# A hybrid mLSTM and attention block on one core: sweep order of the input projection, gate sums moved to TensorE, head norms moved to VectorE

## The chip, the cores and the metric

The kernel runs on one core of a Trainium2 chip. A core has TensorE (PE in the profile; its weight loads are PEld), VectorE (DVE), ScalarE (ACT), GpSimd (POOL) and a queue engine SyncE (SP), which here issues every DMA. All weights lie in HBM in float32 and are read once per launch, 313.81 MB in all. The metric is the device time of one launch in microseconds; smaller is better. Times are given as the median of several executions. One further execution was profiled.

## The reference

One transformer-like layer on 256 tokens of width 2048, in float32:

```
mod = silu(c) @ w_ada + b_ada -> shift1, scale1, gate1, shift2, scale2, gate2   (each 2048 wide)
h   = rms_norm(x, norm1_w) * (1 + scale1) + shift1
mq, mk, mv, mo, mi, mf, dq, dk, dv = split(h @ w_in)
h_ml = rms_norm(mlstm_chunkwise(silu(conv(mq)), silu(conv(mk)), mv, gates(mi, mf))) * sigmoid(mo)   (4 heads)
dq, dk = rope(rms_norm(dq)), rope(rms_norm(dk))
o_da = rms_norm(diff_attention(dq, dk, dv, lam))      (8 heads, two softmax maps each)
x = x + gate1 * (concat(h_ml, o_da) @ w_out)
h = rms_norm(x, norm2_w) * (1 + scale2) + shift2
g, u = split(h @ w_gate_up);  x = x + gate2 * ((silu(g) * u) @ w_down)
```

The kernel computes the mLSTM of a head as one masked 256 x 256 product with a running maximum. Nothing of what is computed differs between the two versions but the order of sums and the way a reciprocal root is refined.

## The kernel before

**Ticks.** The large products are cut into 392 ticks. A tick is 256 rows by 512 columns of weights, 0.524 MB. ACT makes the high part `wh` (line 542), DVE the rest `wl = raw - wh` (line 552), and TensorE runs 12 products of 512 columns, three for each of two weight rows blocks and two token halves: high by high, high by low, low by high (lines 581 to 583). The input projection takes 96 ticks, the output projection 32, the gate and up projection 176, the down projection 88. The order of the ticks is fixed when the program is made.

**Sweeps.** The input projection has 12 column groups: `DQ`, `DK`, `DV` with two groups each, `MQ`, `MK` with one each, `MV`, `MO` with two each. A group needs eight steps of 256 rows, and step p needs `h0_p`, the normed and modulated piece p of x, which in turn needs the column pair p of scale1 and shift1. So the groups are not done one by one but in sweeps (lines 48 to 55): all 12 groups for step 0, all for step 1, ten groups for steps 2 and 3 (`LATE[FIRST:]` leaves out `DV`), then the six `EARLY` groups for steps 4 to 7, `DV` for steps 2 to 7, and the other four for 4 to 7. At the end of every visit to a group, `project_done` (line 680) copies the accumulator to `proj` (ACT, first visit) or adds it (DVE).

**The modulation.** `w_ada` is read in 192 tiles of 128 x 1024 (0.524 MB), 32 for each of the six parts, through four buffers (`NADA`). A tile is summed in one of two ways. On DVE, it is multiplied with silu(c) and summed in one instruction (line 366). On TensorE, four products at four column positions of the array run beside each other (line 346), and after four tiles of a column pair p, `finish` (line 349) copies the row with ACT and turns it into a column by two tiny products `gc`. `on_pe` (line 38) chooses: in the version before, part 1 (scale1) for six of eight pairs and part 0 (shift1) for pairs 0 to 3 are on TensorE; all else is on DVE, part 2 (gate1) too. The tiles' order is `items` (line 302): pairs of parts 1 and 0, then part 2, then pairs of parts 4 and 3 (scale2, shift2), then part 5 (gate2). `ADA_PLAN` (line 1413) says how many tiles are due in which sweep and how many ticks ahead of its end; `due` (line 1261) makes a number per tick of it. `ada_idle` (line 372) uses tiles earlier where the plan sees them landed and DVE or TensorE with room. The last 32 tiles are held back until the last gate-up stretch (`ada_limit`).

**The small work.** Everything else (making `h0_p`, norms and rotation of queries and keys in `prep`, attention heads in `attend` and `attend_values`, `finish_attention`, the memory heads in `ml_scores` and `ml_values`, the gate rows in `gate_rows`) is written as generators. Each `yield` ends a step and tells how many of four PSUM banks the next one needs. `Plan.run` (line 138) goes through them in order at every half tick and issues one step of each, as long as its running estimate of DVE's and ACT's queued work, `v` and `a`, is under 2.3 us. `Plan.until` issues what a tick needs before its products are issued. All engines then run their instructions in that order, so an instruction that has to wait holds up those behind it on its engine.

**Steps that the change touches.** `prep` makes 16 reciprocal roots per token row by a first guess on DVE and three Newton rounds on POOL (`rsqrt_newton`, line 399, four POOL instructions a round); `finish_attention` and `ml_norm` use it too, with `yield 0` twice behind it. `attend` takes the maximum of a head's scores on DVE, scales it on POOL (line 785), yields, and takes the exponential on ACT (line 793). `ml_scores` yields between maximum (line 953) and exponential (line 956).

**The end of the input projection.** The output projection takes groups 0 and 1 with the attention's parts `mix2`, `mix3` first, then with the memory parts `mix0`, `mix1`. A group's end there needs `rows1`, the rows of gate1 that `gate_rows` spreads to 128 partitions (`g1rd` on DVE, `g1rp` on TensorE, four times).

Of the kernel before, what the change touches and what calls it, by code (L numbers as in the profile page):

```python
# [27 lines left out]
NADA = 4  # L28
# [9 lines left out]
def on_pe(s, p):  # L38
    return (s == 1 and p % 3 != 2) or (s == 0 and p < PE0)

# [4 lines left out]
VMAX = AMAX = 2.3  # L45
VADA = 1.8

DQ, DK, DV, MQ, MK, MV, MO = (0, 1), (2, 3), (4, 5), 6, 7, (8, 9), (10, 11)
EARLY = (DQ[0], DK[0], MQ, MK, DQ[1], DK[1])
LATE = (DV[0], DV[1], MV[0], MV[1], MO[0], MO[1])  # L50
FIRST = 2
SWEEPS = (
    (EARLY + LATE, 0, 1), (EARLY + LATE, 1, 2), (EARLY + LATE[FIRST:], 2, 4), (EARLY, 4, 8),
    (LATE[:FIRST], 2, 8), (LATE[FIRST:], 4, 8),
)
# [34 lines left out]
class Plan:  # L90
# [47 lines left out]
    def run(self, force=False, only=None):  # L138
        for w in list(self.works):
            if only is not None and w.name not in only:  # L140
                continue
            if not force and (self.v > VMAX or self.a > AMAX):
                break
            if w.last + (w.need > 0) >= self.now or w.need > self.free or not all(self.ok(x) for x in w.after):
                continue
            self.free -= w.need
            w.last = self.now
            try:
                w.need = next(w.gen)
            except StopIteration:  # L150
                self.works.remove(w)
                self.mark(w.name)
# [12 lines left out]
def tile_block(ctx, tc, x, c, pos, par, w_ada, w_in, w_gt, w_out, w_gu, w_dn, out):  # L165
# [147 lines left out]

    ada_limit = [len(items) - 32]

    def ada_dma(n=None):
        while ada_next[0] < ada_limit[0] and ada_next[0] < ada_next[1] + NADA and (n is None or n > 0):
            s, p, q = items[ada_next[0]]
            t = sl.tile([P, 1024], F32, name=f"ada{s}_{p}_{q}", tag="ada", bufs=NADA)
            nc.sync.dma_start(t[:], w_ada[s, p, q])  # L320
            ada_tiles[s, p, q] = t
            ada_ready.append(plan.load(0.5))
            ada_next[0] += 1
            n = None if n is None else n - 1

    def ada_batch():

        s, p, _ = items[ada_next[1]]
        return 2 if on_pe(s, p) else 1

    def ada_use():
        s, p, q = items[ada_next[1]]
        n = ada_batch()
        while ada_next[0] < ada_next[1] + n:
            ada_dma(1)
        ts_ = [ada_tiles.pop((s, p, q + y)) for y in range(n)]
        t = ts_[0]
        if on_pe(s, p):
# [5 lines left out]
            for y, t in enumerate(ts_):  # L344
                for j in range(4):
                    mm(pg[32 * j:32 * j + 32, :256], scol[:, (q + y) * 4 + j, :], t[:, j * 256:(j + 1) * 256],
                       q + y == 0, q + y == 3, passes=1.2, tile_position=(0, 32 * j))
            if q == 2:
                def finish():
# [22 lines left out]
    def ada_idle(vmax=VADA):  # L372
        while ada_next[1] < ada_next[0]:
            last = ada_next[1] + ada_batch() - 1
            if last >= ada_next[0] or ada_ready[last] > plan.t:
                break
# [4 lines left out]
            elif plan.v > vmax:  # L381
                break
            ada_dma(ada_use())

# [14 lines left out]
    def rsqrt_newton(y, b, x_):  # L399
        for _ in range(3):  # L400
            nc.gpsimd.tensor_tensor(b, y, y, op=ALU.mult)
            nc.gpsimd.tensor_tensor(b, b, x_, op=ALU.mult)
            nc.gpsimd.tensor_scalar(b, b, -0.5, 1.5, op0=ALU.mult, op1=ALU.add)
            nc.gpsimd.tensor_tensor(y, y, b, op=ALU.mult)

# [322 lines left out]
    def prep(nm, g):  # L728
# [12 lines left out]
        if nm == "q":  # L741
            nc.gpsimd.tensor_scalar(dst, dst, 0.125, None, op0=ALU.mult)
            rope_products(nm, t)
# [21 lines left out]
    def attend(h):  # L765
# [18 lines left out]
        scale = sclq[:, :, h * 2:h * 2 + 2]  # L784
        nc.gpsimd.tensor_tensor(st[:, :, 2:4], st[:, :, 0:2], scale, op=ALU.mult)  # L785
        yield 0
        work = slab(f"pm{h}")
# [43 lines left out]
    def finish_attention(g):  # L831
# [7 lines left out]
        rsqrt_newton(f, b, xx)  # L839
        yield 0  # L840
        yield 0
# [82 lines left out]
    def ml_scores(h):  # L924
# [27 lines left out]
        for t, o, w, do in parts:  # L952
            red(mneg[:, h, t:t + 1], L[:, o:o + w + 1], ALU.max, negate=True)
        yield 0
        for t, o, w, do in parts:
# [36 lines left out]
    def ml_norm(g):  # L992
# [7 lines left out]
        rsqrt_newton(mf[:, h], mfb[:, h], mfx[:, h])  # L1000
        yield 0
        yield 0
# [258 lines left out]
    def due(i):  # L1261
        n = 8
        for a, b, k in loads:
            n += k * min(max(i + 1 - a, 0), b - a) / (b - a)
        a, b = spans["fr"]
        if i >= a + 4:
            n = len(items) - 32 + 32 * (i - 3 - a) / (b - 24 - a)
        return min(int(n + 1e-6), len(items))
# [10 lines left out]
    plan.free -= 1  # L1279
    for n in range(2):  # L1280
        ada_dma(ada_use())
        next(h0)
    next(h0)
    nc.sync.dma_start(gw, w_gt[:, :])
    nc.sync.dma_start(lamt, par[:, NPAR - 256:])
    weights_dma(1)
    for n in range(2):
        for _ in range(2):
            plan.next_half()
            plan.run(force=True)  # L1290
        ada_dma(ada_use())
    weights_dma(1)
    while "ada0_0" not in plan.done:
# [58 lines left out]
    for i, t in enumerate(ticks):  # L1352
# [10 lines left out]
        weights_dma()  # L1363
        if i == spans["fr"][0]:
            ada_limit[0] = len(items)
            ada_dma()
        while ada_next[1] < due(i):
            ada_dma(ada_use())
        ada_dma()
# [42 lines left out]

ADA_PLAN = ((0, 12, 3), (1, 16, 4), (2, 28, 0), (3, 8, 0), (4, 4, 0), (5, 4, 0), ("wo", 16, 22), ("f0", 24, 5), ("f1", 32, 5), ("f2", 8, 8))

# [70 lines left out]
```

## Time and profile before

| | |
|---|---|
| median of three executions | 1232.72 us (1229.62 to 1233.36) |
| the profiled execution: time, span | 1227.86 us, 1226.1 us |
| TensorE busy | 1189.7 us, 97% |
| DVE, ACT, POOL busy | 851.1, 582.1, 50.4 us |
| w_ada sums on DVE | 152, 1.217 us each |
| w_ada sums on TensorE | 40 tiles (320 matmul records) |
| POOL instructions | 126 |
| read from HBM | 310.73 MB, 255 GB/s over the span |

A row of the timeline gives start, length, engine, line, operation, output and inputs, shapes, count, and in brackets the idle time of the engine before it with what ended it. Buffer numbers are left out of names; `acc('in', 3, 2)` is the accumulator of group 3 of the input projection in the visit that begins with step 2. A row of the stretches gives the stretch, its length, then busy time and instruction count of each engine, the granted clock of TensorE as a share of full speed, the busy share of the DMA engines, and GB/s. Busy times of TensorE overlap, since one product is in flight while the next starts.

### The profile page before, as it was taken

The numbers are of one execution on the slowest core, as the hardware profiler recorded it, in microseconds if no ns is written. First come the engines' busy times: TensorE is split into PE (matmuls) and PEld (weight loads), VectorE is DVE, ScalarE is ACT, GpSimd is POOL, SyncE is SP. The second block draws the span as 40 slices with busy tenths as digits, with TensorE's granted clock in tenths as the row PEclk, the third lists the DMA queues.
The fourth block names the chain that finished last, engine by engine and source line by source line (L and its number), as shares of the span: only waits on it lengthen the run. The fifth ranks groups of instructions, "written<-read, shape, count | busy, mean of one in ns | idle before, by whom it ended". The sixth has DMA issues, their size and how long they took to land.

```text
span 1226.1 us, 14849 instructions
## 1 busy us (share of the span) xinstructions
PE 1189.7 (97%) x5590; PEld 955.9 (78%) x5590; DVE 851.1 (69%) x1197; ACT 582.1 (47%) x791; POOL 50.4 (4%) x126
## 2 busy tenths in 40 slices
PE   6999899998999898999999999999999999999998
PEld 2767678777888686788888888888888878888886
DVE  3757968898888998879856667878555454545443
ACT  3754345565666345665444444444444443433342
POOL 1000001205022000000000000000000000000000
PEclk9999999999999999999999999999999999999999
DMA  9898987656578897899755547998655544646471
GB/s 343 320 363 321 376 324 251 252 207 234 183 257 314 315 355 279 307 337 344 276 186 184 188 169 291 353 351 319 233 178 196 189 172 172 225 169 238 157 257 52
DMA packets 63258, 313.81 MB, mean 256 GB/s; under 512 B 6993, under 2 KB 7377, under 8 KB 41169
## 3 DMA queue, kind: packets, MB, share of 16 engines
q1 hardware_dynamic: 63186, 312.86, 69.9%
q8 instruction: 44, 0.72, 0.2%
q14 instruction: 28, 0.23, 0.0%
HBM read 310.73 MB, written 2.10 MB: 255 GB/s over the span
## 4 chain that ended last, share of the span: by engine, by line
PE 77%; DVE 13%; issue 3%; DMA 2%; POOL 2%; ACT 2%; SPq 0%; DVEq 0%; POOLq 0%; ACTq 0%
DVE wl L181 5%; DVE ada L185 4%; DMA ada<-in_w_ada_dram 2%; PE acc('dn', 0)_7816 L583 2%; PE acc('dn', 0)_7816 L581 2%; PE acc('dn', 2)_8616 L583 2%; PE acc('dn', 2)_8616 L581 2%; PE acc('dn', 1)_8236 L583 2%; PE acc('dn', 1)_8236 L581 2%; PE acc('dn', 0)_7816 L582 2%; PE acc('dn', 2)_8616 L582 2%; PE acc('dn', 1)_8236 L582 2%; DVE proj L181 1%; PE gv L216 1%; PE at L220 1%
## 5 line engine op out<-in xcount | busy, mean ns | idle before, releaser
L181 DVE TENSOR_TENSOR wl<-r,wh 128x1024 fp32r<-128x1024 f32 x392 | 473.6, 1221 | 206.6 <-ACT wh L211 206.3
L211 ACT ACTIVATE wh<-r 128x1024 fp32r<-128x1024 f32 x392 | 410.5, 1058 | 391.3 <-DMA r<-in_w_gu_dram 42.1
L185 DVE SCALAR_TENSOR_TENSOR ada<-ada,silc 128x1024 f32<-128x1024 f32 x152 | 183.0, 1217 | 1.7 <-DMA ada<-in_w_ada_dram 1.7
L216 PE MATMUL gv<-ada,early 128*32 128x256 f32 x320 | 25.7, 424 | 11.9 <-DMA ada<-in_w_ada_dram 11.7
L581 PE MATMUL acc('dn', 0)_7816<-wh,aTh 128*128 128x512 f32 x88 | 35.9, 408 | 0.0
L583 PE MATMUL acc('dn', 0)_7816<-wh,aTl 128*128 128x512 f32 x88 | 34.3, 390 | 0.0
L582 PE MATMUL acc('dn', 0)_7816<-wl,aTh 128*128 128x512 f32 x88 | 34.3, 389 | 0.0
L581 PE MATMUL acc('dn', 1)_8236<-wh,aTh 128*128 128x512 f32 x88 | 34.2, 389 | 0.0
L582 PE MATMUL acc('dn', 1)_8236<-wl,aTh 128*128 128x512 f32 x88 | 34.2, 389 | 0.0
L583 PE MATMUL acc('dn', 1)_8236<-wh,aTl 128*128 128x512 f32 x88 | 34.2, 389 | 0.0
L581 PE MATMUL acc('dn', 2)_8616<-wh,aTh 128*128 128x512 f32 x88 | 34.2, 389 | 0.0
L582 PE MATMUL acc('dn', 2)_8616<-wl,aTh 128*128 128x512 f32 x88 | 34.2, 389 | 0.0
L583 PE MATMUL acc('dn', 2)_8616<-wh,aTl 128*128 128x512 f32 x88 | 34.2, 389 | 0.0
L216 PEld LDWEIGHTS gv<-ada,early 128*32 128x32 f32 x320 | 7.8, 113 | 27.3 <-DMA ada<-in_w_ada_dram 16.4
L211 ACT ACTIVATE hx<-pt,modc,gcol 128x256 f32<-128x256 f32 (+1 forms) x36 | 17.4, 535 | 17.7 <-PE pt L220 14.6
L181 DVE TENSOR_TENSOR hl<-hx,hh 128x512 fp32r<-128x512 f32 (+1 forms) x18 | 11.4, 631 | 18.8 <-ACT hh L211 18.7
L211 ACT ACTIVATE pm<-sc,st,sclq 128x256 f32<-128x256 f32 (+1 forms) x32 | 15.9, 513 | 12.0 <-POOL st L785 12.0
L211 ACT ACTIVATE aTh<-at 128x512 fp32r<-128x512 f32 x22 | 12.0, 596 | 20.0 <-PE at L220 20.0
L211 ACT ACTIVATE fp<-fp 128x1024 f32<-128x1024 f32 x6 | 6.4, 1062 | 29.4 <-DVE fp L181 29.4
L582 PEld LDWEIGHTS acc('dn', 0)_7816<-wl,aTh 128*128 128x128 f32 x88 | 16.5, 188 | 4.2 <-issue 1.0
L581 PEld LDWEIGHTS acc('dn', 0)_7816<-wh,aTh 128*128 128x128 f32 x88 | 16.5, 188 | 4.2 <-issue 1.0
L582 PEld LDWEIGHTS acc('dn', 2)_8616<-wl,aTh 128*128 128x128 f32 x88 | 16.5, 188 | 3.5
(958 smaller groups left out, 2985.9 us busy)
## 6 DMA issues: line engine op xcount, KB each, us to landing
ada<-in_w_ada_dram SPq DMA_DIRECT2D x192, 512.0 KB, 5.7
r<-in_w_gu_dram SPq DMA_DIRECT2D x76, 1024.0 KB, 6.3
r<-in_w_dn_dram SPq DMA_DIRECT2D x44, 1024.0 KB, 4.8
r<-in_w_in_dram SPq DMA_DIRECT2D x36, 1024.0 KB, 6.7
r<-in_w_out_dram SPq DMA_DIRECT2D x16, 1024.0 KB, 7.4
r<-in_w_in_dram SPq DMA_DIRECT2D x24, 512.0 KB, 5.9
r<-in_w_gu_dram SPq DMA_DIRECT2D x24, 512.0 KB, 4.3
x<-in_x_dram SPq DMA_DIRECT2D x4, 512.0 KB, 5.9
```

Of the source, the lines that this page charges most:

```text
L181: nc.vector.tensor_tensor(o, a, b, op=op)
L185: nc.vector.scalar_tensor_tensor(out=o, in0=a, scalar=s, in1=b, op0=op0, op1=op1, accum_out=accum)
L211: nc.scalar.activation(o, a, func, **kw)
L216: nc.tensor.matmul(o, l, r, start=start, stop=stop, **kw)
L220: nc.tensor.transpose(o, a, ident[:])
L581: nc.tensor.matmul(o, ah[:, s], wh[:, r], start=t["start"] and j == 0, stop=False)
L582: nc.tensor.matmul(o, ah[:, s], wl[:, r], start=False, stop=False)
L583: nc.tensor.matmul(o, al[:, s], wh[:, r], start=False, stop=t["stop"] and j == 1)
```

## The change

It has five parts. (1) The third sweep of the input projection visits all 12 groups again; the two `MO` groups then do steps 4 and 5, the six `EARLY` groups steps 4 to 7, `DV` and `MV` steps 4 to 7, `MO` steps 6 and 7. The due numbers of the w_ada tiles follow, and the hold on the last 32 tiles goes. (2) Part 2 of w_ada (gate1) is summed on TensorE, only when all four tiles of a column pair are there; the other TensorE sums take what is due, one to four tiles. (3) The Newton rounds run on DVE in three instructions instead of four on POOL. (4) The maximum's scaling is on DVE, and maximum and exponential are issued in one step, for both kinds of heads; one `yield` less stands behind the norms. (5) Work that has begun may go on until the estimates reach 4.8 us instead of 2.3, and the plan passes over work that is stopped instead of ending its round there.

```diff
 def on_pe(s, p):
-    return (s == 1 and p % 3 != 2) or (s == 0 and p < PE0)
+    return (s == 1 and p % 3 != 2) or s == 2 or (s == 0 and p < PE0)
...
+VMORE = 2.5
...
-FIRST = 2
+FILL = 2
 SWEEPS = (
-    (EARLY + LATE, 0, 1), (EARLY + LATE, 1, 2), (EARLY + LATE[FIRST:], 2, 4), (EARLY, 4, 8),
-    (LATE[:FIRST], 2, 8), (LATE[FIRST:], 4, 8),
+    (EARLY + LATE, 0, 1), (EARLY + LATE, 1, 2), (EARLY + LATE, 2, 4), (LATE[6 - FILL:], 4, 6),
+    (EARLY, 4, 8), (LATE[:6 - FILL], 4, 8), (LATE[6 - FILL:], 6, 8),
 )
...
-            if not force and (self.v > VMAX or self.a > AMAX):
-                break
+            more = VMORE if w.last >= 0 else 0.0
+            if not force and (self.v > VMAX + more or self.a > AMAX + more):
+                continue
...
-    ada_limit = [len(items) - 32]
-
     def ada_dma(n=None):
-        while ada_next[0] < ada_limit[0] and ada_next[0] < ada_next[1] + NADA and (n is None or n > 0):
+        while ada_next[0] < len(items) and ada_next[0] < ada_next[1] + NADA and (n is None or n > 0):
...
-    def ada_batch():
-
-        s, p, _ = items[ada_next[1]]
-        return 2 if on_pe(s, p) else 1
-
-    def ada_use():
+    def ada_batch(limit, ready):
+
         s, p, q = items[ada_next[1]]
-        n = ada_batch()
-        while ada_next[0] < ada_next[1] + n:
-            ada_dma(1)
+        n = 0
+        while ada_next[1] + n < min(limit, ada_next[0]) and n < (4 - q if on_pe(s, p) else 1) and (
+                not ready or ada_ready[ada_next[1] + n] <= plan.t):
+            n += 1
+        return 0 if s == 2 and n < 4 else n
+
+    def ada_use(n=1):
+        s, p, q = items[ada_next[1]]
...
     def ada_idle(vmax=VADA):
         while ada_next[1] < ada_next[0]:
-            last = ada_next[1] + ada_batch() - 1
-            if last >= ada_next[0] or ada_ready[last] > plan.t:
+            n = ada_batch(len(items), True)
+            if n == 0:
                 break
...
     def rsqrt_newton(y, b, x_):
         for _ in range(3):
-            nc.gpsimd.tensor_tensor(b, y, y, op=ALU.mult)
-            nc.gpsimd.tensor_tensor(b, b, x_, op=ALU.mult)
-            nc.gpsimd.tensor_scalar(b, b, -0.5, 1.5, op0=ALU.mult, op1=ALU.add)
-            nc.gpsimd.tensor_tensor(y, y, b, op=ALU.mult)
+            tt(b, y, y, ALU.mult)
+            stt(b, b, -0.5, x_, ALU.mult, ALU.mult)
+            stt(y, b, 1.5, y, ALU.add, ALU.mult)
...
-            nc.gpsimd.tensor_scalar(dst, dst, 0.125, None, op0=ALU.mult)
+            ts(dst, dst, 0.125, None, ALU.mult)
...
-        nc.gpsimd.tensor_tensor(st[:, :, 2:4], st[:, :, 0:2], scale, op=ALU.mult)
-        yield 0
+        tt(st[:, :, 2:4], st[:, :, 0:2], scale, ALU.mult)
...
         rsqrt_newton(f, b, xx)
         yield 0
-        yield 0
...
             red(mneg[:, h, t:t + 1], L[:, o:o + w + 1], ALU.max, negate=True)
-        yield 0
...
         rsqrt_newton(mf[:, h], mfb[:, h], mfx[:, h])
         yield 0
-        yield 0
...
-        a, b = spans["fr"]
-        if i >= a + 4:
-            n = len(items) - 32 + 32 * (i - 3 - a) / (b - 24 - a)
...
         while ada_next[1] < due(i):
-            ada_dma(ada_use())
+            n = ada_batch(due(i), False)
+            if n == 0:
+                break
+            ada_dma(ada_use(n))
...
-ADA_PLAN = ((0, 12, 3), (1, 16, 4), (2, 28, 0), (3, 8, 0), (4, 4, 0), (5, 4, 0), ("wo", 16, 22), ("f0", 24, 5), ("f1", 32, 5), ("f2", 8, 8))
+ADA_PLAN = ((0, 12, 3), (1, 16, 4), (2, 24, 3), (3, 4, 0), (4, 16, 0), (5, 12, 0), (6, 4, 0), ("wo", 16, 22), ("f0", 24, 5), ("f1", 32, 5), ("f2", 24, 8))
```

At the start, the first eight tiles are used one at a time instead of two.

More of the change, by code (lines that the diff above doesn't have):

```diff
@@ L347, in ada_use @@
                        q + y == 0, q + y == 3, passes=1.2, tile_position=(0, 32 * j))
-            if q == 2:
+            if q + n == 4:
                 def finish():
@@ L1279, in tile_block @@
     plan.free -= 1
-    for n in range(2):
+    for n in range(4):
         ada_dma(ada_use())
-        next(h0)
-    next(h0)
+        if n < 3:
+            next(h0)
     nc.sync.dma_start(gw, w_gt[:, :])
@@ L1286, in tile_block @@
     weights_dma(1)
[L1287 to L1290, printed above, removed]
+    for n in range(4):
         ada_dma(ada_use())
+        plan.next_half()
+        plan.run(force=True)
     weights_dma(1)
@@ L1363, in tile_block @@
         weights_dma()
-        if i == spans["fr"][0]:
-            ada_limit[0] = len(items)
-            ada_dma()
         while ada_next[1] < due(i):
-            ada_dma(ada_use())
+            n = ada_batch(due(i), False)
+            if n == 0:
+                break
+            ada_dma(ada_use(n))
         ada_dma()
```

## The prediction

> **What bounds the kernel now.** I read the page first, then the stretches of the stages, then the spacing of the weight products, then who TensorE waited for.
>
> ```profile
> PE 1189.7 (97%) x5590; PEld 955.9 (78%) x5590; DVE 851.1 (69%) x1197; ACT 582.1 (47%) x791; POOL 50.4 (4%) x126
> ```
>
> TensorE is the busiest engine, but its busy time overlaps itself, so the spacing of its products says more than the 97%. Two first products of neighbouring output groups, 264 products apart:
>
> ```profile
> 1041.83 0.39 PE L581 MATMUL acc('dn', 1)_8236<-wh,aTh 128*128 128x512 f32 x1
> ...
> 1101.67 0.39 PE L581 MATMUL acc('dn', 2)_8616<-wh,aTh 128*128 128x512 f32 x1
> ```
>
> 59.84 us / 264 = 0.2267 us a product, so a tick (12 products) takes 2.72 us when nothing disturbs it. 392 ticks make 1066 us of the span of 1226.1 us, whatever the other engines do. The rest is small work on TensorE and waiting. Where is the waiting? The stretches are: first two sweeps, third sweep, rest of the input projection, output projection, first sweep of the feed-forward, everything behind it.
>
> ```profile
> 28.00:116.00 88.00, 87.93 (x518) 64.93 (x519) 58.35 (x107) 49.65 (x66) 0.00 (x0) 0.97 0.92 341
> 116.00:187.00 71.00, 64.29 (x325) 49.06 (x324) 57.70 (x83) 28.76 (x37) 0.00 (x0) 0.98 0.90 333
> 187.00:379.00 192.00, 185.03 (x940) 151.16 (x939) 167.17 (x325) 116.12 (x248) 41.30 (x94) 0.99 0.65 231
> 379.00:482.00 103.00, 97.27 (x421) 77.35 (x419) 94.79 (x147) 50.10 (x73) 5.79 (x12) 0.98 0.90 343
> 482.00:554.00 72.00, 69.16 (x310) 56.08 (x311) 56.88 (x97) 46.51 (x64) 0.00 (x0) 1.00 0.80 298
> 554.00:1226.00 672.00, 667.51 (x2984) 551.02 (x2982) 408.46 (x421) 280.39 (x290) 0.00 (x0) 1.00 0.62 222
> ```
>
> Columns: length, then busy time of PE, PEld, DVE, ACT, POOL, clock, DMA share, GB/s. Behind 554 us TensorE idles under 5 us in 672, at the tail. So nothing that the change moves there (the last 32 w_ada tiles come earlier, out of the last gate-up stretch) can shorten it, and DVE at 408 of 672 has room for it. All that can be won lies ahead of 554 us, and the view of TensorE's waits names it (total, times, longest):
>
> ```profile
> PE gv L216 <- DMA ada<-in_w_ada_dram: 11.7, 13, 1.9
> PE ot L220 <- DVE o L181: 4.2, 1, 4.2
> ...
> PE g1rp L216 <- DVE g1rd L181: 3.5, 1, 3.5
> PE acc('gu', 0, 0)_4206 L581 <- ACT hh L211: 2.2, 2, 1.1
> PE acc('gu', 4, 0)_4423 L582 <- DVE wl L181: 1.3, 2, 1.0
> PE pt L220 <- DVE hx L190: 1.3, 1, 1.3
> PE tpk L220 <- DVE proj L181: 1.3, 1, 1.3
> PE aT L220 <- ACT pm L211: 0.7, 1, 0.7
> ```
>
> Of the 11.7 us on w_ada, some 5 belong to the start, which the change leaves alone but for the order of eight single sums. About 22 us of waits remain. A long wait costs more than itself, since the clock drops behind it (here the columns are length, PE, clock, DMA):
>
> ```profile
> 306.00:310.00 4.00, 3.10 (x17) 0.57 0.54 225
> ...
> 419.00:423.00 4.00, 4.00 (x9) 0.58 0.96 378
> ```
>
> 0.57 and 0.58 over 4 us are 1.7 us each on top of the 4.2 and the 3.5. Behind the waits on w_ada near 162 us the drop is of the same kind (I take 1.7 again). So the pool is about 22 + 5 = **27 us**.
>
> **What the change adds.** Gate one's 32 tiles go from DVE to TensorE. An existing sum of two tiles, between two weight products:
>
> ```profile
> 47.47 0.39 PE L583 MATMUL acc('in', 1, 0)_451<-wh,hl 128*128 128x512 f32 x1
> 47.79 1.07 PE L216 MATMUL gv<-ada,early 128*32 128x256 f32 x16
> 48.79 0.50 PE L581 MATMUL acc('in', 3, 0)_500<-wh,hh 128*128 128x512 f32 x1
> 49.13 0.40 PE L582 MATMUL acc('in', 3, 0)_500<-wl,hh 128*128 128x512 f32 x1
> ...
> 103.58 0.39 PE L583 MATMUL acc('in', 8, 1)_983<-wh,hl 128*128 128x512 f32 x1
> 103.81 0.50 PE L216 MATMUL gc<-ones,gr 128*128 128x1 f32 x4
> 104.17 0.63 PE L220 MATMUL pt<-ident,hx 128*128 128x128 f32 x4
> ```
>
> From 47.47 to 49.13 are 1.66 us where two spacings would be 0.45: two tiles cost 1.2 us, of which about 0.3 is the turn between kinds of product. Four tiles in one go are 4 x 0.45 + 0.3 = 2.1 us. Behind each column pair come the turning products gc, 0.36 us and about 0.1 of turning. That is 2.56 us for each of eight column pairs, **+20.5 us** on the engine that bounds the kernel, in a stretch where it is nearly always busy. From below: two pairs without their turn, 8 x (1.8 + 0.36) = 17.3; from above, no saving of fours over twos, 8 x (2.4 + 0.5) = 23.2.
>
> The sums of the first two matrices now go by what is due, one or two at a time instead of always two: some five more turns at 0.3, less what falls into waits: **+1 us** (0 to 1.5).
>
> **What it takes away.** (1) *Third sweep.* It has 24 ticks instead of 20, and 24 tiles due in 21 ticks instead of 28 in 20. Traffic a tick falls from 2.4 to 2.14 pieces of 0.524 MB.
>
> ```profile
> 140.00:145.00 5.00, 2.46 (x22) 1.06 (x21) 5.00 (x8) 1.06 (x1) 0.00 (x0) 1.00 0.99 360
> 145.00:150.00 5.00, 3.31 (x20) 2.05 (x19) 3.32 (x3) 1.06 (x1) 0.00 (x0) 1.00 0.98 388
> ```
>
> Here the DMA engines are full at 360 to 388 GB/s, and DVE is full too (5.00 of 5.00), so buffers come free late. At 374 GB/s a tick needs 3.37 us of DMA before and 3.0 after, against 2.72 us of products. The first tile of pair 6 is due 2.1 ticks (5.7 us) later, in which 2.1 more weight pieces take 2.9 us of DMA: 2.8 us won of its waits. Pair 7 is due 3.4 ticks (9.2 us) later for 4.8 us of DMA: its 2.3 us of waits go, and some of the cold clock. Together **-6 us** (bounds 0 and -9: all 6.6 us of waits, some turning and the cold clock).
>
> (2) *Norms.* The wait of 4.2 us for `o` comes from POOL:
>
> ```profile
> 300.07 0.22 POOL L404 TENSOR_TENSOR rstk<-rstk,rsk 128x16 f32<-128x16 f32 x1
> 300.25 0.20 POOL L401 TENSOR_TENSOR of<-of 128x8 f32<-128x8 f32 x1
> ...
> 305.39 0.20 POOL L404 TENSOR_TENSOR of<-of 128x8 f32<-128x8 f32 x1
> ...
> 281.98 0.17 DVE L192 TENSOR_SCALAR rsq<-rsq 128x16 f32<-128x16 f32 x1
> 282.19 0.17 DVE L190 TENSOR_SCALAR rsq<-rsq 128x16 int32<-128x16 int32 x1
> ```
>
> The norm stood behind the key norm until 300.25 and then took 5.3 us. On DVE it is nine instructions at about 0.2 us (the two last rows, start to start), 1.9 us. The wait goes with its cold clock: **-5.5 us**. `tpk` waited for the same reason: **-1.4 us**. The waits around `pm` (POOL scaled the maximum): **-0.5 us**. What DVE takes over is 8 norms x 9 x 0.2 + 10 single ones = 16 us, and four more accumulations into `proj` at 1.2 = 5 us.
>
> Against that stands what leaves DVE:
>
> ```profile
> 187.00:379.00 192.00, 38.66 (x64) 0.99 0.65 231
> 379.00:482.00 103.00, 36.28 (x60) 0.98 0.90 343
> ```
>
> These are the w_ada sums alone on DVE: 32 of them (and 32 short reads) took 38.7 us in the 192. DVE was 87% busy there (167 of 192) and falls to about 77% (167 - 39 + 16, less the `wl` of 8 ticks that now lie earlier, over some 175 us).
>
> (3) *Output projection.* `g1rp` waited 3.5 us, because DVE ran w_ada sums between the four steps of the gate's rows. With gate one off DVE, and started work allowed 2.5 us more of planned DVE load, I expect the rows ahead of their need: **-4.5 us** of 3.5 + 1.7. (4) The two waits on `wl` in the feed-forward: **-1 us**. The waits on `hx` and `hh` (3.5 us) are the turn itself and stay.
>
> (5) *What is late next.* The query and key groups end at tick 76 of 96, not 68; 20 ticks are left for two attention groups and four memory heads. And the exponentials now stand in ACT's queue directly behind a maximum that DVE has not made; behind them wait the next `wh`, then `wl`, then the products. I price this between 0 and two waits like that for `o` (2 x 5.9), and take half of one: **+3 us**.
>
> Sum: 20.5 + 1 - 6 - 5.5 - 1.4 - 0.5 - 4.5 - 1 + 3 = **+5.6 us**. The profiled execution took 1227.86 us (span 1226.1), so 1233.5; the median shown is 1232.72, 4.9 above the profiled one, so the forecast for the median is **1238 us**.
>
> [...]
>
> **The rivals.** *A: faster.* Nearly all of the pool goes, 25 of 27 us, with no new wait, at the lower price of the sums: 17.3 + 1 - 25 = -6.7, **1226 us**. For it: DVE loses 39 us just where it is fullest, and the planner's limits are loosened. Against: waits on DMA are only lightened. It decides itself by whether step 1 is worth 9 rather than 6 and step 5 nothing.
>
> *B: a wash.* Of the pool 20 to 22 us go against 21.5 of cost: **1233 us**. It needs the forecast without step 5 (+2.6) and a little more won in the third sweep.
>
> *C: much slower.* The second attention group reaches the output projection late.
>
> ```profile
> 293.20 1.14 DVE rsk L196
> ...
> 382.27 1.32 DVE odl L185 x2
> ```
>
> From the second key reduction to its last output part the chain took 89 us. The need is now 22 ticks behind the last key group: at 192 us / 52 ticks = 3.69 us a tick 81 us, and three new sums 7.7: 89. It just fits if the reduction starts at once. Before, it started 24 us behind the key group, and a norm on DVE returns only 3.4 of it. With half of the remaining 20 us late, the sum is 2.6 + 10 = +12.6, **1245 us**.
>
> *D: the change does not do what it says:* fours that never gather in four buffers would be summed only when due, and gate rows wait for them at tick 107. That ends like C, and I count it there.
>
> **How the numbers follow.** Chances: forecast 0.37, A 0.29, B 0.24, C (with D) 0.10. A measurement here tells about 0.3% (3.7 us) from no change: faster is A, the same is B, slower is the forecast and C: 0.29, 0.24, 0.47. The range leaves out a little of A's end and half of C: 1224 to 1246. Cases of both signs hold most of the chance; the forecast's own range is 1236 to 1243.
>
> **What would show it.** Right: eight sums of x32 with about 2.1 us each between 200 and 380 us; waits on w_ada in the third sweep near 3 us; no wait for `o`, `tpk` or `g1rp` over 1 us; pace 0.2267 behind the first feed-forward sweep. Wrong for the sums: if a four costs under 1.8 us, or falls where TensorE waits anyway. Wrong for the chain: idle TensorE over 4 us at the start of the output projection is C. Waits on w_ada gone altogether, with no new ones, are A.

## The result, and the profile after

| | before | after |
|---|---|---|
| median | 1231.17 us (1229.38 to 1233.36, four runs) | 1240.47 us (1240.12 to 1241.04, four runs) |
| profiled execution: time, span | 1227.86 us, 1226.1 us | 1240.26 us, 1238.5 us |

The ratio is 1.0075, with a 95% interval of 1.0054 to 1.0096: the change makes the kernel **9.3 us slower**. The two profiled executions differ by more, 12.4 us, because that of before lay 3.3 us under its median. The ledger below is made of these two.

The first part of the page of after, in the columns of before's:

```profile
PE 1211.5 (98%) x5878; PEld 966.7 (78%) x5878; DVE 836.1 (68%) x1225; ACT 588.5 (48%) x801; POOL 3.3 (0%) x20
```

TensorE has 288 more matmul records (256 are the eight new sums of four tiles, 32 products each, and 32 their turning products). DVE has 15 us less work, POOL is practically empty.

The stretches of after, cut at the same times as before's:

```profile
116.00:187.00 71.00, 70.59 (x359) 54.27 (x358) 62.67 (x84) 31.99 (x40) 0.00 (x0) 1.00 0.92 346
187.00:379.00 192.00, 187.44 (x1137) 146.25 (x1137) 145.44 (x337) 111.33 (x234) 0.00 (x0) 0.99 0.66 239
379.00:482.00 103.00, 99.48 (x446) 82.17 (x447) 92.98 (x157) 54.67 (x87) 0.00 (x0) 0.98 0.82 304
```

Between 116 and 187 us TensorE now is busy for 70.6 of 71 us (64.3 before), with DMA traffic still at 346 GB/s. From 187 to 379 us DVE falls from 167 to 145 us. So both reliefs that the change makes arrive. What they bring is read from the stages. A stage is bounded here by the first product of its first visit; these rows of the timeline bound them, first before, then after:

```profile
186.87 0.39 PE L581 MATMUL acc('in', 0, 4)_1621<-wh,hh 128*128 128x512 f32 x1
...
379.06 0.48 PE L581 MATMUL acc('wo', 0)_3396<-wh,odh 128*128 128x512 f32 x1
...
482.38 0.50 PE L581 MATMUL acc('gu', 0, 0)_4206<-wh,hh 128*128 128x512 f32 x1 [1.08 <-ACT hh L211]
...
553.57 0.48 PE L581 MATMUL acc('gu', 0, 2)_4790<-wh,hh 128*128 128x512 f32 x1
```

```profile
204.90 0.39 PE L581 MATMUL acc('in', 0, 4)_1771<-wh,hh 128*128 128x512 f32 x1
...
397.19 0.39 PE L581 MATMUL acc('wo', 0)_3600<-wh,odh 128*128 128x512 f32 x1
...
494.97 0.50 PE L581 MATMUL acc('gu', 0, 0)_4349<-wh,hh 128*128 128x512 f32 x1 [1.08 <-ACT hh L213]
...
564.16 0.39 PE L581 MATMUL acc('gu', 0, 2)_4937<-wh,hh 128*128 128x512 f32 x1
```

| stage | before | after | difference |
|---|---|---|---|
| up to the `EARLY` groups, step 4 | 186.9 us, 44 ticks | 204.9 us, 52 ticks | +18.0, of which 8 ticks are 21.8: **-3.8** |
| from there to the output projection | 192.2 us, 52 ticks | 192.3 us, 44 ticks | +0.1 with 21.8 us less of products: **+21.9** |
| output projection | 103.3 us | 97.8 us | **-5.5** |
| first feed-forward sweep | 71.2 us | 69.2 us | **-2.0** |
| the rest | 672.5 us | 674.3 us | **+1.8** |

The sum is +12.4, the difference of the spans. TensorE's waits in after (total, times, longest) tell what stands behind the stages:

```profile
PE gv L218 <- DMA ada<-in_w_ada_dram: 3.6, 7, 1.3
PE ot L222 <- DVE o L183: 3.5, 1, 3.5
PE cvt L222 <- ACT pm L213: 2.5, 2, 2.2
...
PE gv L218 <- ACT pm L213: 0.9, 1, 0.9
PE acc('gu', 5, 5)_6042 L582 <- DVE wl L183: 0.8, 1, 0.8
...
PE sc L218 <- ACT pm L213: 0.7, 1, 0.7
PE acc('gu', 7, 5)_6177 L582 <- DVE wl L183: 0.7, 1, 0.7
...
PE tpq L222 <- DVE proj L183: 0.5, 1, 0.5
```

(A helper of before at L181, L211 or L220 stands two lines lower in after.) The waits on w_ada fell from 11.7 to 3.6 us (in the third sweep alone from 6.6 to 0.4), and `g1rp` and `tpk` are gone. The waits on `pm` grew from 1.2 to 4.1 us. And `ot` waits for `o` again, at another place: at the very start of the output projection, where the second attention group is needed.

### The profile page after: what moved, and what is told of

Same layout as the page of the kernel before. It is cut to its first block, busy times and chain, and to the rows that moved or that the text cites. A ratio compares the mean times of both kernels' runs of the same rounds, so it can differ in the third digit from the quotient of the medians.

```text
span 1238.5 us, 15369 instructions
## 1 busy us (share of the span) xinstructions
PE 1211.5 (98%) x5878; PEld 966.7 (78%) x5878; DVE 836.1 (68%) x1225; ACT 588.5 (48%) x801; POOL 3.3 (0%) x20
## 4 chain that ended last, share of the span: by engine, by line
PE 87%; DVE 5%; DMA 3%; ACT 2%; issue 1%; SPq 0%; ACTq 0%; DVEq 0%
PE gv L218 3%; DVE wl L183 2%; DMA ada<-in_w_ada_dram 2%; PE acc('dn', 0)_7950 L583 2%; PE acc('dn', 0)_7950 L582 2%; PE acc('dn', 1)_8370 L582 2%; PE acc('dn', 2)_8750 L582 2%; PE acc('dn', 2)_8750 L581 2%; PE acc('dn', 1)_8370 L581 2%; PE acc('dn', 0)_7950 L581 2%; PE acc('dn', 1)_8370 L583 2%; PE acc('dn', 2)_8750 L583 2%; DMA r<-in_w_gu_dram 1%; DVE ada L187 1%; PE apart('dn', 3)_9131 L582 1%
## 5 line engine op out<-in xcount | busy, mean ns | idle before, releaser
L187 DVE SCALAR_TENSOR_TENSOR ada<-ada,silc 128x1024 f32<-128x1024 f32 x120 | 145.0, 1217 | 0.0
L581 PE MATMUL acc('dn', 0)_7950<-wh,aTh 128*128 128x512 f32 x88 | 36.0, 409 | 0.0
L583 PE MATMUL acc('dn', 0)_7950<-wh,aTl 128*128 128x512 f32 x88 | 34.3, 390 | 0.0
L582 PE MATMUL acc('dn', 0)_7950<-wl,aTh 128*128 128x512 f32 x88 | 34.3, 390 | 0.0
L581 PE MATMUL acc('dn', 1)_8370<-wh,aTh 128*128 128x512 f32 x88 | 34.3, 389 | 0.0
L583 PE MATMUL acc('dn', 2)_8750<-wh,aTl 128*128 128x512 f32 x88 | 34.3, 389 | 0.0
L582 PE MATMUL acc('dn', 1)_8370<-wl,aTh 128*128 128x512 f32 x88 | 34.3, 389 | 0.0
L583 PE MATMUL acc('dn', 1)_8370<-wh,aTl 128*128 128x512 f32 x88 | 34.3, 389 | 0.0
L581 PE MATMUL acc('dn', 2)_8750<-wh,aTh 128*128 128x512 f32 x88 | 34.2, 389 | 0.0
L582 PE MATMUL acc('dn', 2)_8750<-wl,aTh 128*128 128x512 f32 x88 | 34.2, 389 | 0.0
L183 DVE TENSOR_TENSOR hl<-hx,hh 128x512 fp32r<-128x512 f32 (+1 forms) x18 | 11.4, 631 | 12.3 <-ACT hh L213 12.2
```

The lines of the kernel that those rows point to most:

```text
L183: nc.vector.tensor_tensor(o, a, b, op=op)
L187: nc.vector.scalar_tensor_tensor(out=o, in0=a, scalar=s, in1=b, op0=op0, op1=op1, accum_out=accum)
L581: nc.tensor.matmul(o, ah[:, s], wh[:, r], start=t["start"] and j == 0, stop=False)
L582: nc.tensor.matmul(o, ah[:, s], wl[:, r], start=False, stop=False)
L583: nc.tensor.matmul(o, al[:, s], wh[:, r], start=False, stop=t["stop"] and j == 1)
```

## The experiments

All times are medians; the ratio to before comes with its 95% interval. In these sessions before took 1231.6 to 1232.5 us.

### Is it the sums? One part put back, one cost cut

**gate1_on_dve.** Theory: the sums on TensorE are the loss, and with gate one back on DVE the rest of the change wins. From after:

```diff
 def on_pe(s, p):
-    return (s == 1 and p % 3 != 2) or s == 2 or (s == 0 and p < PE0)
+    return (s == 1 and p % 3 != 2) or (s == 0 and p < PE0)
...
-        return 0 if s == 2 and n < 4 else n
+        return n
```

> The changed kernel with gate one's 32 tiles summed on VectorE again; sweeps, due numbers, norms, one-step maximum and exponential all stay. Theory 1 (the sums' own TensorE time is the loss): the eight sums with their gc took 8 x (1.86 + 0.36) = 17.8 us and some 2 of turning; DVE gets 39 us back in a stretch where it was busy 145 of 192, so a few waits return: 1240 falls by 10 to 18, to 1222-1230 us, below both kernels at best. Rival (the loss is the shortened time for the attention and memory heads, the sums only fill waits): falls by less than 4, 1236 or more, with the wait for o at the start of the output projection still there.

Measured: 1276.06 us, 1.036 (1.0336 to 1.0385), 36 us worse than after. The theory fell, by far. In the timeline the groups 4, 5, 8 and 9 (and 6 before them) take 10.88 us each, 48 products at 0.2267 and nothing else: TensorE gets no head's work for long stretches. Two stretches of this run, the visits to groups 5, 8 and 9, and the first visit of the output projection (length; PE, PEld, DVE, ACT, POOL; clock, DMA share, GB/s):

```profile
296.61:329.26 32.65, 32.65 (x145) 27.04 (x144) 32.65 (x46) 14.69 (x16) 0.00 (x0) 1.00 0.91 343
...
368.89:439.75 70.86, 45.68 (x209) 35.34 (x207) 49.73 (x165) 29.34 (x92) 0.00 (x0) 0.74 0.28 98
```

In the first, DVE is busy for all of 32.65 us and TensorE runs at its pace. The heads' work then has to be done all at once: the first visit of the output projection lasts 70.9 us instead of 13.2, at a clock of 0.74, and TensorE waits for the chain of the heads:

```profile
PE ot L222 <- DVE o L183: 11.2, 2, 6.0
```

So the new due numbers, which put 28 gate-one tiles into two sweeps, are more than DVE can take beside the rest; the next run takes them away. That the plan began no head there because its estimate of DVE's queue stood above its limit is read from the code, not shown.

**gate1_on_dve_late.** The same edit, with before's spread of those tiles (8, 4, 4 due in the last three sweeps, 16 in the last gate-up stretch):

> The changed kernel with gate one's 32 tiles on VectorE again, as in gate1_on_dve, but with few of them due in sweeps 4 to 7 (8, 4, 4 instead of 16, 12, 4; the last 16 of all in the last gate-up stretch), as the version before had it; more of them may still come early where VectorE has room. Theory 1 (gate1_on_dve lost its 36 us because forced sums kept the planner's VectorE estimate over its limit, so that no new head was begun; the sums' TensorE time is what the change costs): the heads run again, the 18 to 20 us of sums are saved and some waits return: 1222-1232 us. Rival (VectorE has no room for these tiles beside norms and heads in the 20 ticks left, whenever they are due): 1240 us or more, with waits on DVE or ACT over 5 us at the output projection.

Measured: 1261.66 us, 1.0247 (1.0227 to 1.0267). The output projection starts at 395.2, 2 us earlier than in after, but then waits 7.9 us on `g1rp` and runs its third visit in 30.0 us instead of 10.9. That is 14 us better than with the new due numbers, but still, with DVE doing the sums, the other parts of the change cost 30 us.

**short_sums.** After, with three of the four tiles of a gate-one pair summed over 32 of 256 columns only:

```diff
-                    mm(pg[32 * j:32 * j + 32, :256], scol[:, (q + y) * 4 + j, :], t[:, j * 256:(j + 1) * 256],
+                    w = 32 if s == 2 and q + y > 0 else 256
+                    mm(pg[32 * j:32 * j + 32, :w], scol[:, (q + y) * 4 + j, :], t[:, j * 256:j * 256 + w],
```

> The changed kernel; of gate one's sums, three of the four tiles of each column pair are summed in 32 of their 256 columns only (the rest is left out), in the same order and with the same waits. Theory 1: a tile of 256 columns costs 0.45 us, one of 32 about 0.1: 24 x 0.35 = 8 us less, 1232 us. Rival (the sums lie in time in which TensorE would wait anyway): within 2 us of 1240.

Measured: 1234.51 us, 1.002 (1.0007 to 1.0032): 6.0 us less than after. The busy time of all sums between 187 and 379 us, after and then this run (columns PE, PEld, ACT; clock, DMA share, GB/s):

```profile
187.00:379.00 192.00, 15.47 (x256) 7.51 (x256) 3.05 (x8) 0.99 0.66 239
```

```profile
187.00:379.00 192.00, 6.61 (x256) 4.35 (x256) 3.07 (x8) 0.99 0.68 249
```

8.9 us of products taken out bring 6.0. So about two thirds of this TensorE time are paid in the kernel's time; a part of the rest turns into waits (`sc` on `pm` 1.8 instead of 0.7, `tpq` 1.3 instead of 0.5).

### The parts alone, on the kernel before

**before_gate1_on_pe.** Before with `or s == 2` in `on_pe` and nothing else; the sums then go in twos.

> The version before with one edit: gate one's 32 tiles summed on TensorE, in twos. Theory 1: 16 twos at 1.2 us and 8 gc at 0.46 are 23 us more on TensorE; the relief of VectorE takes away the wait for g1rp (5.5 us) and little else: 1245-1252 us. Rival (VectorE is what holds up that stretch): 1236 us or less.

Measured: 1239.37 us, 1.0066 (1.0051 to 1.0081), +7.8 us, less than the 23 that the sums in twos were priced at. From 188.2 us to the output projection it takes 213.7 us instead of 192.2, but the output projection then takes 92.0 us instead of 103.3. From its table of waits:

```profile
PE gv L216 <- DMA ada<-in_w_ada_dram: 6.7, 10, 1.9
...
PE tpk L220 <- DVE proj L181: 0.5, 1, 0.5
```

`ot` on `o` and `g1rp` are gone and `tpk` is nearly so, **with the norms still on POOL**. Moving the sums off DVE (142.8 us busy from 187 to 379 instead of 167.2) is by itself enough to end them.

**before_third_sweep.** Before with the new sweeps and their due numbers (24, 4, 8, 4, 4) only.

> The version before with the order of the sweeps and their due numbers alone (24, 4, 8, 4, 4 due in sweeps 3 to 7), gate one on VectorE, norms on GpSimd. Theory 1: the steps up to tick 52 end near 205 us instead of 187 + 22 = 209 (4 to 8 us won on w_ada waits), and the eight ticks fewer for the heads give as much or more back: 1228-1240 us. Rival (the later query and key groups cost nothing as the planner's limit, not the groups, sets the heads' pace): 1227 us or less.

Measured: 1240.66 us, 1.0076 (1.0053 to 1.0099). Up to step 4 of the `EARLY` groups it gains 6.6 us (202.1, where 186.9 and 8 ticks would be 208.7), and then loses more: the first visit of the output projection takes 46.7 us instead of 13.2.

```profile
PE acc('wo', 0)_3243 L583 <- DVE odl L185: 9.7, 1, 9.7
```

That is the mechanism of the rival "much slower", the attention late at the output projection, as long as DVE does the sums; its price is +9 us where the prediction had 12.6.

**before_norms_dve_one_step.** Before with part (3) and all of part (4).

> The version before with two edits: the Newton rounds and the scalings on VectorE instead of GpSimd, and maximum and exponential in one step. Theory 1: the waits for o (5.9 us with the cold clock) and tpk (1.4) go, 16 us more on VectorE and the exponentials behind the maximum give 2 to 4 back: 1227-1231 us. Rival (VectorE, 87% busy there, has no room): 1234 us or more.

Measured: 1249.54 us, 1.0149 (1.0125 to 1.0173), +18 us, where a gain had been expected. The wait that grew most is that on gate one's rows; the first row is from the table of waits, the others are DVE's instructions between two of its four steps, from the timeline:

```profile
PE g1rp L216 <- DVE g1rd L181: 10.4, 4, 3.4
```

```profile
426.53 0.69 DVE L181 TENSOR_TENSOR g1rd<-ident,modc 128x512 f32<-128x512 f32 x1
427.14 1.22 DVE L185 SCALAR_TENSOR_TENSOR ada<-ada,silc 128x1024 f32<-128x1024 f32 x1
...
430.57 0.68 DVE L181 TENSOR_TENSOR g1rd<-ident,modc 128x512 f32<-128x512 f32 x1
```

From 427.14 to 430.57 DVE does three w_ada sums of 1.22 us, one begun as the one before ends, between two steps; the next `g1rp` on TensorE waits for the second step.

**before_all_norms_dve.** The same without the one step: all Newton rounds, the scalings of the queries (`dst`) on DVE and one `yield` less behind them, the maximum still scaled on POOL and followed by a `yield`.

> The version before with all Newton rounds and the query scaling on VectorE (and one yield less behind two of them), but the maximum's scaling on GpSimd and maximum and exponential in two steps as before. It divides the 18 us that before_norms_dve_one_step lost. If the one step is the cost (exponentials waiting in ACT's queue): 1217-1226 us, like before_one_norm_dve. If the norms of queries, keys and memory heads are (80 small instructions that the planner counts at half their length, on an engine 87% busy): 1235-1249 us.

Measured: 1231.5 us, 0.9997 (0.9984 to 1.001), the time of before. So in before the one step, together with the maximum's scaling on DVE that came with it, is what costs the 18 us, and the norms together are worth nothing. The traces of the two runs put most of that cost ahead of the output projection, not at `g1rp`: from the `EARLY` groups to there the run with the one step takes 198.2 us, this one 185.0; the output projection then takes 118.2 and 110.8. Against before, the norms do win time in the first of these stages (192.2 there), but the output projection gives it back (103.3 in before), and so does the stretch behind the first feed-forward sweep (676.4 us, 672.5 in before).

**before_one_norm_dve.** Before, with only the norm in `finish_attention` on DVE, the one whose result `ot` waited for; the other three users of `rsqrt_newton` stay on POOL:

```diff
+    def newton_dve(y, b, x_):
+        for _ in range(3):
+            tt(b, y, y, ALU.mult)
+            stt(b, b, -0.5, x_, ALU.mult, ALU.mult)
+            stt(y, b, 1.5, y, ALU.add, ALU.mult)
...
-        rsqrt_newton(f, b, xx)
+        newton_dve(f, b, xx)
```

> The version before with the Newton rounds of finish_attention alone on VectorE (18 instructions, about 3 us); gate one on VectorE, sweeps, query, key and memory norms as before. If the wait of 4.2 us for o came from standing behind the key norm on GpSimd alone: 5.9 us less, 1225-1228 us, faster than both. Rival (any load on VectorE there moves the heads later and the waits with them, as with all norms): 1231 us or more.

Measured: **1216.75 us** (1215.69 to 1217.84), 0.9882 (0.9863 to 0.9902), 15 us faster than before and 24 faster than after (the profiled executions of before and this run are 12.2 us apart). The last Newton round on DVE, the product `o` and what is left of the wait, from the timeline:

```profile
300.13 0.37 DVE L185 SCALAR_TENSOR_TENSOR of<-of 128x8 f32<-128x8 f32 x2
...
303.36 1.22 DVE L181 TENSOR_TENSOR o<-o,of 128x1024 f32<-128x1024 f32 x1
...
304.63 1.09 PE L220 MATMUL ot<-ident,o 128*128 128x128 f32 x8 [1.19 <-DVE o L181]
```

`o` starts at 303.4 instead of 305.6, and `ot` waits 1.2 us instead of 4.2. The wait on `g1rp` is gone too, in a stage that the edit doesn't touch. By stage, from the profiled executions: from the `EARLY` groups to the output projection 185.6 us (192.2), the output projection 98.8 (103.3), the first feed-forward sweep 69.0 (71.2).

### The parts taken out of after

**two_steps.** After with the `yield` between maximum and exponential back in `attend` and `ml_scores`.

> The changed kernel with the yield between maximum and exponential put back for both kinds of heads (the scaling stays on VectorE). Theory 1: the 4.4 us of waits that the trace of after puts on ACT pm (cvt, gv, sc) go, but each head takes half a tick more: 1236-1239 us, and the wait for o at the output projection stays or grows. Rival (one step is what saves the chain): slower than 1240 by 2 or more.

Measured: 1246.83 us, 1.0123 (1.0098 to 1.0148), +6.4 against after. The waits on `pm` change (`cvt` goes, `sc` waits 2.4 us), but `tpq` waits 4.4 us in all. The one step is worth 6 us in after, where with the scaling it costs 18 in before. Not all of the 6 are the heads': of the 6.1 us between the two profiled executions 3.4 lie behind the first feed-forward sweep, where no head is left (TensorE's waits on `wl` and `fp` there are 3.8 us, 1.5 in after), so they belong to the order that the plan arrived at.

**norms_on_pool.** After with all Newton rounds and the scaling of the queries on GpSimd again, and the `yield`s behind the norms.

> The changed kernel with the Newton rounds on GpSimd again (with the second yield behind two of them); the scaling of the maximum stays on VectorE. The prediction's step 2 holds: the waits for o and tpk return, 5 to 8 us slower than 1240, 1245-1248 us. Rival (the waits for o and tpk came from VectorE's load and the queue on GpSimd, and with the sums off VectorE they are gone either way, as the version before with gate one on TensorE shows): 1236-1242 us.

Measured: 1240.19 us, 1.0068 (1.005 to 1.0087), the time of after. Two of the waits for which the norms had been blamed are longer than in after:

```profile
PE ot L222 <- DVE o L183: 4.3, 1, 4.3
...
PE tpk L222 <- DVE modc L183: 0.8, 1, 0.8
```

That is 0.8 us more each (after has 3.5 and none). With the sums off DVE, the place of the norms makes no difference to the time.

**old_sweeps.** After with before's sweeps (due 28, 16, 6, 10).

> The changed kernel with the sweeps of before (28, 16, 6, 10 due in sweeps 3 to 6, gate one on TensorE in fours). The prediction's steps 1 and 5: the waits on w_ada in the third sweep return (tick 52 at 209 us instead of 205), and the wait of 3.5 us for o at the output projection with its cold clock goes, as query and key groups end 8 ticks earlier: 1237-1242 us. Rival (the third sweep is a plain gain of 6 to 8 us once VectorE has room): 1244-1248 us.

Measured: 1247.08 us, 1.0127 (1.0104 to 1.0149), +6.6. `gv` waits 7.4 us on w_ada again (3.6 in after). So the new sweeps are worth 6.6 us in after, but only a part of it arises where the prediction looked for it: the `EARLY` groups start at 185.9 us with 44 ticks, which makes 207.7 with eight more, against 204.9, so 2.7 us. In the third sweep this run waits 2.4 us on w_ada, after 0.4. The rest comes later, where the small work lies otherwise (`gc` waits 3.5 us on ACT, `po` 1.8).

**start_in_twos.** After with the start's eight single sums, and the later ones, in twos.

> The changed kernel with the start as before: the first eight tiles two at a time, and in the first sweeps TensorE's sums in twos also where only one is due. Theory 1: tick 12 begins at 70.2 us in before and 74.7 in after, all of it from the single sums at the start: 4 us less, 1236 us. Rival (the 4.5 us is a shift by the DMA that the third sweep gives back, so nothing is won): within 1.5 us of 1240.

Measured: 1239.31 us, 1.0066 (1.0043 to 1.0088), 1.2 us under after, which is within the noise. The second sweep starts 2.4 us earlier (72.2 against 74.7), but the `EARLY` groups start at 205.4 (204.9 in after): `gv` waits 6.8 us on w_ada instead of 3.6. The start's delay is one that the transfers give back: the 2.4 us won at the start return as one wait of 2.4 us on w_ada in the third sweep.

## Why the prediction was right, and where its steps were not

The forecast was slower by 5.6 us, the medians say 9.3. That its 1238 us comes within 2.5 us of the measured median is in part luck. It added 4.9 us because the profiled execution of before lay that far below its median; that of after lies only 0.2 us below its own, so these 4.9 us stand in for most of the 6.8 by which the terms fall short of the profiled pair (12.4). By its own terms, against that pair:

| step | forecast | measured in the traces |
|---|---|---|
| eight sums of four, with `gc` | +20.5 | +20.2 |
| finer batches at the start | +1 | +4.2 |
| (1) third sweep | -6 | -7.9 |
| (2) `o`, `tpk`, `pm` of before | -5.5, -1.4, -0.5 | -5.9, -1.3, -1.2 |
| (3) `g1rp` | -4.5 | -5.2 |
| (4) `wl` in the feed-forward | -1 | -2.0 and +1.8 |
| (5) what is late next | +3 | +11.5 |

The measured column makes +14.2, 1.8 us more than the spans differ by. It is worked out so: the start by the first product of the third sweep (119.8 us against 115.7), the third sweep by its distance to the `EARLY` groups without the 8 added ticks, waits by the tables of waits with 1.7 us for each stretch of lowered clock (0.57 or 0.58 over 4 us, 0.66 over 5), (4) by the last two rows of the stages, and (5) as 3.5 + 1.7 for `ot`, 4.1 + 1.7 for `pm` and 0.5 for `tpq`. The column is a ledger of waits, not a proof of each entry. By stages its terms make +18.1 from the `EARLY` groups to the output projection, where +21.9 were measured, and nothing in the output projection, where -5.5 were measured. Some small work changed stage, which explains a part: the products `g1rp` and the last `nu` run ahead of the output projection in after, 3 us by their spacing, and one `ot` of 1.3 us went the other way. What makes the rest was not traced.

**The sums** were priced right. A row of four tiles in after between two products:

```profile
218.41 0.39 PE L583 MATMUL acc('in', 0, 4)_1771<-wh,hl 128*128 128x512 f32 x1
218.72 1.93 PE L218 MATMUL gv<-ada,early 128*32 128x256 f32 x32
220.59 0.50 PE L581 MATMUL acc('in', 2, 4)_1900<-wh,hh 128*128 128x512 f32 x1
220.93 0.40 PE L582 MATMUL acc('in', 2, 4)_1900<-wl,hh 128*128 128x512 f32 x1
...
242.36 0.39 PE L583 MATMUL acc('in', 6, 4)_2020<-wh,hl 128*128 128x512 f32 x1
242.59 0.50 PE L218 MATMUL gc<-ones,gr 128*128 128x1 f32 x4
242.95 0.48 PE L581 MATMUL acc('in', 6, 4)_2020<-wh,hh 128*128 128x512 f32 x1
243.26 0.39 PE L582 MATMUL acc('in', 6, 4)_2020<-wl,hh 128*128 128x512 f32 x1
```

218.41 to 220.93 are 2.52 us where two spacings are 0.45: 2.07, forecast 2.1. For `gc` it is 0.90 - 0.45 = 0.45, forecast 0.46. Eight times both are 20.2 us. That most of this time is paid is what short_sums showed: 6.0 us for 8.9.

**The start and the third sweep.** Twelve ticks in, after is 4.5 us behind, foreseen as 1; the third sweep then wins 7.9 instead of 6. start_in_twos shows that the two belong together, so they are to be read as one: -3.8, forecast -5. The mechanism of (1) was right as far as the waits go: those of the third sweep fall from 6.6 to 0.4 us and its clock stays full (1.00 from 120 to 205 us in after), 7.9 us together (the prediction had named waits near 3 us as its sign). How much of it is due to the order of the sweeps depends on the rest: with the old sweeps and all else of after the same stretch is already 5.0 us shorter than in before (66.3 us, 71.2), perhaps because the transfers catch up during the slower start, which was not traced.

**Norms: the cause was wrong.** The prediction put the waits for `o` and `tpk` down to POOL's norms. They did go, but before_gate1_on_pe loses them but for 0.5 us with the norms left on POOL, and norms_on_pool is as fast as after. The wait for `o` is one for a chain that runs through DVE's queue as well as POOL's: before_all_norms_dve is rid of it too, so either relief ends it, and the second one then brings nothing. For `tpk` the reason was wrong altogether, since with its norm on DVE it still waits 1.5 us in before_all_norms_dve. The terms of (2) match because each wait was counted once, but in after the gain can't be credited to the norms. On the kernel before, the step as written, all norms on DVE, is worth nothing. The one norm alone gets 15 us, where the terms for `o`, `g1rp` and `wl` add up to 11; that the last two waits would go with it was not foreseen.

**(3)** `g1rp`'s wait of 3.5 us is gone with its cold clock (0.58 over 4 us in before): 3.5 + 1.7. **(4)** The waits on `wl` left the first feed-forward sweep (1.3 us in all in before), and two of 0.7 and 0.8 came up in the third, where the last 32 w_ada tiles now also lie: the prediction had no term behind 554 us, and it is 1.8 us.

**(5) is the term that was mis-sized**, 11.5 instead of 3. Of its two reasons the first held: the second attention group was late at the output projection. The timeline of after there:

```profile
401.19 1.21 DVE L183 TENSOR_TENSOR proj<-proj,acc('in', 11, 6)_3516 128x1024 f32<-128x1024 f32 x1
402.32 1.22 DVE L183 TENSOR_TENSOR o<-o,of 128x1024 f32<-128x1024 f32 x1
...
403.59 1.60 PE L222 MATMUL ot<-ident,o 128*128 128x128 f32 x8 [3.52 <-DVE o L183]
```

and its clock around it (length; PE, PEld, DVE, ACT, POOL; clock, DMA share, GB/s):

```profile
400.00:404.00 4.00, 0.48 (x5) 0.41 (x5) 3.80 (x10) 0.00 (x0) 0.00 (x0) 1.00 0.90 327
404.00:408.00 4.00, 4.00 (x16) 3.37 (x15) 4.00 (x8) 2.32 (x3) 0.00 (x0) 0.57 0.97 313
```

The norm itself is over on DVE when the first row begins, but `o` stands behind an accumulation of 1.2 us that the plan had queued first. The wait of 3.5 us and 4 us at a clock of 0.57 make 5.2. It is case C in small: 3.5 us idle, where 4 had been named as the mark of C, and it breaks the sign that no wait for `o` would be over 1 us. The clock also fell behind shorter waits, to 0.66 over 5 us, once in before and once in after:

```profile
165.00:170.00 5.00, 5.00 (x23) 3.73 (x15) 2.97 (x4) 0.00 (x0) 0.00 (x0) 0.66 0.88 288
```

```profile
280.00:285.00 5.00, 5.00 (x20) 4.01 (x19) 4.79 (x13) 3.40 (x7) 0.00 (x0) 0.66 0.44 182
```

In before no wait between 140 and 165 us is longer than 1.9 us, and in after the wait ahead of the row is 2.15 us; yet 0.66 over 5 us are 1.7 us lost in each. So the 1.7 us that the prediction took for the third sweep were right. The other reason of (5) holds only in part. It shows on ACT and DVE:

```profile
275.46 0.17 DVE L183 TENSOR_TENSOR st<-st,sclq 128x4 f32<-128x4 f32 x1
275.67 1.05 ACT L213 ACTIVATE wh<-r 128x1024 fp32r<-128x1024 f32 x1
276.73 1.28 ACT L213 ACT_TABLE_LOAD   x1
278.03 0.56 ACT L213 ACTIVATE pm<-sc,st,sclq 128x256 f32<-128x256 f32 x1
...
279.72 1.09 PE L222 MATMUL cvt<-ident,proj 128*128 128x128 f32 x8 [2.15 <-ACT pm L213]
```

The transposes `cvt` wait 2.15 us for the exponentials. The forecast had these wait for a maximum that DVE has not made, but the scaled maximum is there at 275.6: ahead of them on ACT stand a `wh` and a table load of 1.28 us. A late maximum is behind the wait of `sc`, 0.7 us. With `gv` and `cvt`'s other wait it is 4.1 us, and 1.7 of clock; `tpq` adds 0.5. two_steps shows that the one step is nevertheless the better choice in after. It exchanges waits and does not add 4.1 on balance.

**The rivals.** A (nearly all of the 27 us go) and B failed on (5): by the ledger some 23 us of the pool did go, but new waits came, and the sums cost 20.2 us, not A's 17.3. Of C, gate1_on_dve and before_third_sweep show what it costs when DVE keeps the sums: first visits of 70.9 and 46.7 us. D did not happen: all eight sums came as fours.

**Parts do not add up.** Alone on before, the sums cost 7.8, the sweeps 9, the norms 0, one step with the maximum's scaling on top of them 18; together 9.3. Taken out of after, the one step and the sweeps are gains of 6. Without the sums on TensorE the other parts together cost 30 us (gate1_on_dve_late), so it is likely that they need DVE's room, and that this room is what the 20 us on TensorE buy; the looser limit of part (5) is in all runs made from after, and its share can't be told from theirs.

**What stays open.** Why the one step costs 18 us in before and brings 6 in after: the traces show the wait on `g1rp` behind w_ada sums in the one and not in the other, and 13.2 us lost ahead of it, but no run changed either alone. Why one norm on DVE brings 15 us and all of them nothing: up to the output projection both win alike (185.0 and 185.6 us), but in the profiled execution with all of them the output projection takes 110.8 us against 98.8, with `g1rp` waiting 4.7 us. It is likely that the plan orders DVE's work otherwise, as small loads shift its estimates; that was not tested. Part (5) of the change, the plan's looser limit and its passing over of stopped work, was not tried alone, nor was one norm on DVE together with any part of the change.

## What to carry to other kernels

Before moving work, follow the one chain behind the wait: moving only the norm that the largest wait ended on gave 15 us, moving all of them nothing. Where all engines' orders come from one plan, a part's worth is a property of the whole: test each both alone on the old kernel and taken out of the new one, and count a wait as the gain of one part only. Work given to the engine that bounds the kernel costs most of its length (here 6.0 of 8.9 us), and the relieved engine must be worth more than that.

## What was not expected of the hardware

Small POOL instructions beside DVE. In norms_on_pool the timeline has the same kind of instruction on four columns at 0.2 us, and at over a microsecond when it starts beside a `wl` on DVE:

```profile
399.10 1.22 DVE L183 TENSOR_TENSOR wl<-r,wh 128x1024 fp32r<-128x1024 f32 x1
...
399.30 1.07 POOL L405 TENSOR_TENSOR mf<-mf,mfb 128x4 f32<-128x4 f32 x1
400.45 0.21 POOL L402 TENSOR_TENSOR mfb<-mf 128x4 f32<-128x4 f32 x1
```

The long one ends with the DVE instruction (400.37 and 400.32). Beside the accumulation into `proj` on DVE from 397.96 to 399.17 four such instructions on POOL took 0.19 to 0.20 us. The norm of before that took 5.3 us on POOL, with twelve instructions of which the quoted ones take 0.20, is then, by an estimate from these rows, partly a matter of DVE's load: one of the twelve took 1.26 us, from 302.92, beside a `wl` that DVE began at 302.90. How much of the relief comes this way was not measured.
